# Summing the adaLN modulation on ScalarE and GpSimd instead of TensorE, inside the mixers of a two-layer hybrid trunk

## The chip, the cores and the metric

The kernel runs on one core of a Trainium2 chip. Its time is the device time of one execution in microseconds, the median of three runs. A core has TensorE (PE, matrix products; PEld is its loading of weights), VectorE (DVE), ScalarE (ACT), GpSimd (POOL) and SyncE (SP), which here issues the large DMAs. Each engine takes its own instructions in order and waits on semaphores of the others.

## The reference

Two residual layers over a sequence of 256 tokens of width 1024, in fp32, one sequence. Each layer is a mixer (attention of two head groups, one output projection) and a grouped top-2 mixture of 16 experts. Both sub-layers are modulated by a vector c, the same for all tokens:

```
m = silu(c) @ ada_w[layer] + ada_b[layer]          # 1024 x 6144 weights a layer
shift_m, scale_m, gate_m, shift_f, scale_f, gate_f = split(m, 6)
h = rmsnorm(x, norm_mix[layer]) * (1.0 + scale_m) + shift_m
x = x + gate_m * mixer(h)
h = rmsnorm(x, norm_ffn[layer]) * (1.0 + scale_f) + shift_f
x = x + gate_f * grouped_moe(h, ...)
```

The change is about the first line: a product of one row with a 1024 x 6144 matrix, 25 MB of weights a layer, each number of which is used once.

## The kernel before, in words

The program is one long list of instructions for each engine, written by Python generators that take turns, and ordered by a scheduler at build time. It goes through mixer 0, experts 0, mixer 1, experts 1.

The modulation is cut into *parts*. A part is two tiles of 1 MB of `ada_w` (128 partitions x 2048 fp32), loaded by SP into `slot`s, a ring of ten 1 MB tiles that all weights share. `n` is 2 for a shift with its scale (four parts) and 1 for a gate (two parts). The input index is 8 p + k: partition p holds eight rows k of the matrix, and `csil[:, k, 0]` holds silu(c) for them.

Before, `ada_part` gives each part to TensorE: eight matmuls (L340) with one useful column of weights (32 wide, so that four of them stand side by side in the array) and 512 moving columns, accumulated in a PSUM bank, which VectorE then adds to the tile `adac` (L349). `ada_end` closes a sum: for a gate two matmuls spread it over the partitions (L307) and it is added to `GATE`; for a shift and scale eight small matmuls (L313) bring it into columns `MOD` of 128 partitions.

`fill(n)` runs whole parts on the spot (at the start, between the layers, and in the experts). `ada_steps(n, rest)` does them inside a mixer in small steps: it loads one part ahead, lets `rest` steps pass, and then does a part. The attention loop `attend` calls `between()` once in each of its stages, which takes 4 or 5 such steps. There are ten parts in mixer 0 (the gate of its own output, shift and scale of the experts, shift and scale of mixer 1) and four in mixer 1.

In the same stages the side work goes on: projections `proj_t`, `proj_r` (L529 to L531), each k step of which needs a row of weights split into a high and a low part `hl`: ScalarE casts (L514), VectorE or GpSimd subtracts (L471). Then comes the output projection `out_proj`, whose result is added to the residual X (L710, L711). The attention itself uses VectorE for the row minimum (L576) and for weighting (L612, L614), ScalarE for the exponentials (L601).

The router at the start of `moe` finds the experts' order `ex_p`; SP reads it and only then can load the weights of all experts but the first ones.

Of the kernel before, what the change touches and what calls it, by code (L numbers as in the profile page):

```python
# [10 lines left out]
F32 = mybir.dt.float32  # L11
# [12 lines left out]
CAP = 64  # L24
# [83 lines left out]
def trunk(ctx, tc, ins, out):  # L108
# [218 lines left out]
    def ada_part(layer, v, n, j, W):  # L327
# [22 lines left out]
        if j == 2 * n - 1:  # L350
            yield
            ada_end(layer, v, n, sums.pop())

    def fill(n=1):
        for _ in range(n):
            if fills:
                at = fills.pop(0)
                W = first.pop(0) if first else ada_load(*at)
                for _ in ada_part(*at, W):
                    pass  # L360

    def ada_steps(n, rest):

        todo = [fills.pop(0) for _ in range(n)]
        W = ada_load(*todo[0])
# [141 lines left out]
    parts, low = [None], [vec]  # L507
    flop = [0]

    def split(row, n, view=None):  # L510

        t = parts[0].tile([P, 2, 512], F32R, name="hl", tag="hl", bufs=4)
        for src, hi, lo in [(row, t[:, 0, :n], t[:, 1, :n])] if view is None else view(row, t[:, 0, :n], t[:, 1, :n]):
            act.copy(hi, src)  # L514
            flop[0] ^= 1
            split_sub(low[0] or (vec, pool)[flop[0]], lo, src, hi)
        return t[:, 0, :n], t[:, 1, :n]
# [178 lines left out]
            vec.reciprocal(r, r)  # L696
            return [r[:, t:t + 1] for t in range(2)]

    def out_proj(OT, k0, W, engines, norm=None):

        gate = GATE[2]
        o2 = hp.tile([P, 4, 2, S], F32R, name="o2", tag="HT")
        for k in range(4):
            act.copy(o2[:, k, 0, :], OT[:, k0 + k, :])
            split_sub(engines[0], o2[:, k, 1, :], OT[:, k0 + k, :], o2[:, k, 0, :])

        def add(half, t, b):
            sl = slice(half * 512, half * 512 + 512)
            tmp = parts[0].tile([P, 512], F32, tag="tmp", name="tmp")
            vec.tensor_tensor(tmp, b, gate[:, sl], ALU.mult)  # L710
            engines[1].tensor_tensor(X[:, t, sl], X[:, t, sl], tmp, ALU.add)  # L711
            if norm is not None:
                norm.square(t, half)

        for half in range(2):
            outs = [bank("mm", [P, 512]) for _ in range(2)]

            def part(k, t, w):
                mm3(outs[t], [o2[:, k, i, t * P:(t + 1) * P] for i in range(2)], w, k == 0, k == 3)
            sl = slice(half * 512, half * 512 + 512)  # L720
            if half and norm is not None:

                ws = [split(W[k][:, sl], 512) for k in range(4)]
                for t in range(2):
                    for k in range(4):
                        part(k, t, ws[k])
                        yield
                    add(half, t, outs[t])
                continue
            for k in range(4):  # L730
                w = split(W[k][:, sl], 512)
                for t in range(2):
                    part(k, t, w)
                yield
            for t in range(2):
                add(half, t, outs[t])
            if norm is not None and half == 0:
                warm(AF.Sqrt, X[:, 0])


    def even_mixer(big, OT, banks):
# [28 lines left out]
        with scope("evw", 1) as wk:  # L770
# [15 lines left out]
            for i in range(2):  # L786
# [8 lines left out]
                xp = wk.tile([P, 16, 2, 16], F32, tag=f"xp{i}", name="xp")  # L795
# [40 lines left out]
            h1 = wk.tile([32, 512], F32, tag="xp0", name="h1")  # L836
# [137 lines left out]
    def moe(cp, wk, layer, norm, end):  # L974
# [353 lines left out]


        NR = 7  # L1330
        XG_x = cp.tile([P, 8, CAP], F32, name="XG_x")
        w_x = cp.tile([P, 1], F32, name="w_x")
        OT_x = cp.tile([P, 2, 2, P], F32R, name="OT_x")
        sides = [slice(0, 64), slice(64, 128)]

        def x_hidden(XG, W):
# [8 lines left out]
            return hid  # L1345

        def x_slots(o, w):
            def put(tt, wb):
# [3 lines left out]
            by_slot(o, w, 1, put)  # L1352

        def x_transposed(XG, hid):
            hT = XG[:, 4:8, :]
# [5 lines left out]
            act.copy(hT, tb)  # L1361
            return hT

        def x_down(hT, Wd):
            v, yg = row_tiles()
            y = bank("o", [P, 512])
            for k, row in enumerate(Wd):
# [45 lines left out]
        def rounds():  # L1413
# [23 lines left out]
            here, tmp = (cp.tile([P, NR, 16], F32, tag=n, name=n) for n in ("here", "here_t"))  # L1437
            vec.tensor_tensor(here, wide(before), rn, ALU.is_le)
            vec.tensor_tensor(tmp, wide(upto), rn, ALU.is_gt)
            vec.tensor_tensor(here, here, tmp, ALU.mult)  # L1440
# [25 lines left out]
                for i in range(n):  # L1466
                    yield t[:, i, :]

        def round_(i, space, o, XG):

            e = load_value(ex_x[:, i:i + 1], [ET.Pool], NE - 1)
            pick(o, at_x[:, :, i:i + 1].to_broadcast([P, 2, 2]), CAP)
            gather(XG, CAP, o)
            hid = x_hidden(XG, [streamed(nm, e, 8, space) for nm in ("moe_w_gate", "moe_w_up")])
            x_slots(o, wt_x[:, :, i:i + 1])
            for f in x_down(x_transposed(XG, hid), streamed("moe_w_down", e, 4, space)):
                f()

        def rest():
            space = hp.tile([P, 2048], F32, tag="HT", name="space")  # L1480
            o = pick_tile()[:, :, 0:2 * CAP]
            n = load_value(ex_x[:, NR:NR + 1], [ET.PE, ET.Activation, ET.DVE, ET.Pool], NR)

            def go(i):
                if i < NR:
                    with tc.If(n >= i + 1):
                        round_(i, space, o, XG_x)
# [5 lines left out]
        for h in range(2):  # L1493
            vec.tensor_scalar(OT_x[:, h], ident.unsqueeze(1).to_broadcast([P, 2, P]), 0.0, None, ALU.mult)
        then = picked([1, 2], placed[:, 0:2])
        before = None
        for i in range(len(GROUPS)):
# [76 lines left out]
    def odd_mixer(big, wk, OT, banks, CT, CM):  # L1574
# [24 lines left out]

        def put_c(t, b):  # L1600
            evac(VS[:, 0, t, :], b[:, 384:512])
            cl = wk.tile([P, 384], F32, tag="cl", name="cl")
# [153 lines left out]
    with scope("hl0", 2) as parts[0]:  # L1756
        with scope("ev", 1) as e1:
            bias_line()
            banks = norm_transposed()
            fill(4)  # L1760
            ada.add(ada_steps(10, 9))
            OT = new_ot()
            even_mixer(e1, OT, banks)
        wB = load_rows(ins["ev_w_out"][0][512:1024])
# [1 line left out]
        fills += parts_of(0, 5, 1)  # L1766
        norm = Norm()
        router_weights(0)
        run(out_proj(OT, 4, wB, (vec, vec), norm))
    experts(0, norm)  # L1770
    fills += parts_of(1, 2, 1) + parts_of(1, 3, 2)
    fill(2)
    ada.add(ada_steps(4, 9))
    with scope("hl1", 2) as parts[0]:
        with scope("od", 1) as e1, scope("odw", 2) as e2:
            CT, CM, KT[2] = carve((3, S), (256,), (768,))
# [6 lines left out]
        fills += parts_of(1, 5, 1)  # L1783
        norm = Norm()
        router_weights(1)
        run(out_proj(OT, 4, wB, (vec, vec), norm))
    experts(1, norm, Final())


# [23 lines left out]
```

## Time and profile before

| what | us |
|---|---|
| median of 3 runs (range) | 831.33 (828.41 to 831.84) |
| profiled execution | 828.97 |
| its span, first to last instruction | 827.3 |
| TensorE / VectorE / ScalarE / GpSimd busy | 730.9 / 379.0 / 233.7 / 101.0 |
| until 86 us: first modulation, first projections of layer 0 | 86.0 |
| 86 to 201.5: attention and output projection of layer 0 | 115.5 |
| 201.5 to 224: router of layer 0 | 22.5 |
| 224 to 470: experts of layer 0 | 246.0 |
| 470 to 574: mixer 1 | 104.0 |
| 574 to 593: router of layer 1 | 19.0 |
| from 593: experts of layer 1, final norm | 234.3 |

The stages were cut where the instructions of a stage begin. A stage in which one engine is busy nearly all the time goes at that engine's pace; a stage in which the DMA queues move their full rate goes at theirs. A row of the groups reads: line, engine, operation, tile written <- tiles read, shape, count | busy time, mean of one | idle time before it and who ended it.

### The profile page before, as it was taken

What the parts mean: (1) busy time and instruction counts of PE and PEld (TensorE: products, weight loads), DVE (VectorE), ACT (ScalarE), POOL (GpSimd) and SP (SyncE); (2) the same over time, 40 slices, a digit from 0 to 9 for tenths busy, and PEclk for the clock granted to TensorE, in tenths of its full rate; (3) what the DMA queues carried; (4) which work ended last, traced back from release to release, by engine and by line L of the source; (5) the groups of instructions that cost most, each with busy time, mean ns of one, the idle gap of its engine ahead of it and who ended that gap; (6) DMA issues with size and microseconds to landing.
All of it is one profiled execution on the core that took longest, in us unless ns stands there. A gap on an engine that the chain in (4) does not pass through costs nothing. (4 is left out here: it accounts for less than half of the span.)

```text
span 827.3 us, 12080 instructions
## 1 busy us (share of the span) xinstructions
PE 730.9 (88%) x4435; PEld 376.0 (45%) x4435; DVE 379.0 (46%) x1099; ACT 233.7 (28%) x565; POOL 101.0 (12%) x94
## 2 busy tenths in 40 slices
PE   4599999999799997899887899969899988899886
PEld 2298765557433342234222568547443332233223
DVE  2585777777841240312305754885931230322214
ACT  2264555545411110001012455544310110011012
POOL 1020211132200000000001223353100000000001
PEclk9899999999799998999999999998799998999998
DMA  9999878598399999999999987747399999999992
GB/s 355 339 372 418 316 255 256 221 419 321 131 426 374 426 427 424 426 426 427 427 426 414 374 338 210 279 172 279 117 426 377 427 426 423 426 425 428 422 414 91
DMA packets 68457, 291.15 MB, mean 352 GB/s; under 512 B 9174, under 2 KB 23202, under 8 KB 42530
## 3 DMA queue, kind: packets, MB, share of 16 engines
q1 hardware_dynamic: 64048, 283.53, 86.0%
q0 software_dynamic: 1152, 4.21, 1.3%
q10 hardware_dynamic: 3186, 2.51, 0.9%
q8 instruction: 39, 0.64, 0.3%
q14 instruction: 32, 0.26, 0.1%
HBM read 289.16 MB, written 1.06 MB: 351 GB/s over the span
## 5 line engine op out<-in xcount | busy, mean ns | idle before, releaser
L1091 PE MATMUL mm<-slot,XG 128*32 128x512 f32 (+1 forms) x464 | 107.6, 643 | 12.3 <-DMA slot<-in_moe_w_down_dram 6.3
L1091 PE MATMUL o<-slot,hT 128*32 128x512 f32 (+2 forms) x480 | 88.6, 589 | 2.5 <-DMA slot<-in_moe_w_down_dram 2.5
L1118 DVE TENSOR_TENSOR hq<-sc,hid 128x512 f32<-128x512 f32 x14 | 14.7, 1049 | 151.5 <-PE sc L1091 151.5
L514 ACT CAST hl<-slot 128x512 fp32r<-128x512 f32 (+2 forms) x112 | 60.9, 557 | 72.3 <-PE mm L531 41.8
L471 POOL TENSOR_TENSOR hl<-slot,hl 128x512 fp32r<-128x512 f32 x40 | 52.8, 1323 | 158.8 <-ACT hl L514 145.2
L1091 PE MATMUL sc<-slot,XG 128*32 128x512 f32 (+1 forms) x344 | 72.1, 593 | 0.0
L1091 PE MATMUL sc<-room,XG 128*32 128x512 f32 (+1 forms) x296 | 60.7, 593 | 1.2 <-DMA room<-in_moe_w_up_dram 1.2
L1091 PEld LDWEIGHTS mm<-slot,XG 128*32 128x32 f32 (+1 forms) x464 | 27.7, 129 | 69.3 <-issue 67.3
L529 PE MATMUL mm<-HH,hl 128*128 128x256 f32 x176 | 54.2, 310 | 4.7 <-ACT HH L503 4.7
L1162 DVE SCALAR_TENSOR_TENSOR adac<-o,w,GATE 128x512 f32<-128x512 f32 (+1 forms) x29 | 21.2, 732 | 79.0 <-PE o L1091 77.7
L1144 ACT CAST yg<-adac 128x512 fp32r<-128x512 f32 (+1 forms) x28 | 17.1, 612 | 137.9 <-DVE adac L1162 137.9
L1091 PE MATMUL mm<-room,XG 128*32 128x512 f32 (+1 forms) x176 | 52.8, 678 | 0.0
L531 PE MATMUL mm<-HH,hl 128*128 128x256 f32 x176 | 50.0, 286 | 0.8 <-DVE hl L471 0.8
L530 PE MATMUL mm<-HH,hl 128*128 128x256 f32 x176 | 50.2, 287 | 0.0
L471 DVE TENSOR_TENSOR hl<-slot,hl 128x512 fp32r<-128x512 f32 (+2 forms) x72 | 43.3, 623 | 13.5 <-ACT hl L514 13.2
L1091 PE MATMUL o<-room,hT 128*64 128x512 f32 (+2 forms) x176 | 47.4, 577 | 2.2 <-DMA room<-in_moe_w_down_dram 2.0
L340 PE MATMUL tp<-slot,csil 128*32 128x512 f32 x344 | 45.5, 611 | 3.3 <-DMA slot<-in_ada_w_dram 3.1
L1151 PE MATMUL tp<-yg,OT 128*128 128x512 f32 (+1 forms) x112 | 38.1, 441 | 11.1 <-DVE X L1152 5.2
L1073 PE MATMUL tp<-pick,XH 128*128 128x256 f32 (+1 forms) x128 | 39.8, 333 | 8.1 <-DVE XG L1077 4.7
L1152 DVE TENSOR_TENSOR X<-X,tp 128x512 f32<-128x512 f32 (+1 forms) x56 | 36.1, 674 | 17.4 <-PE tp L1151 17.1
L1075 ACT ACTIVATE XG<-tp,mod,mod 128x256 f32<-128x256 f32 (+1 forms) x32 | 17.2, 538 | 94.9 <-PE tp L1073 94.9
L1091 PEld LDWEIGHTS o<-slot,hT 128*32 128x32 f32 (+1 forms) x480 | 24.9, 119 | 40.8 <-issue 34.2
(372 smaller groups left out, 1272.6 us busy)
## 6 DMA issues: line engine op xcount, KB each, us to landing
slot<-in_moe_w_gate_dram SPq DMA_DIRECT2D x48, 1024.0 KB, 13.4
slot<-in_ada_w_dram SPq DMA_DIRECT2D x43, 1024.0 KB, 10.2
slot<-in_moe_w_down_dram SPq DMA_DIRECT2D x42, 1024.0 KB, 19.4
slot<-in_moe_w_up_dram SPq DMA_DIRECT2D x35, 1024.0 KB, 14.4
room<-in_moe_w_up_dram SPq DMA_DIRECT2D x27, 1024.0 KB, 10.1
room<-in_moe_w_down_dram SPq DMA_DIRECT2D x18, 1024.0 KB, 15.3
room<-in_moe_w_gate_dram SPq DMA_DIRECT2D x16, 1024.0 KB, 12.2
slot<-in_ev_w_in_dram SPq DMA_DIRECT2D x8, 1024.0 KB, 8.3
```

The lines of the kernel that those rows point to most:

```text
L340: last[0] = mm(b[32 * g:32 * g + 32], csil[:, k, :], W[i][:, g, :], start=i == 0, stop=i == 1)
L471: return eng.tensor_tensor(lo, v, hi.bitcast(F32), ALU.subtract)
L514: act.copy(hi, src)
L529: mm(o, a[0], b[0], start=start, stop=False, skip_group_check=True)
L530: mm(o, a[0], b[1], start=False, stop=False, skip_group_check=True)
L531: mm(o, a[1], b[0], start=False, stop=stop, skip_group_check=True)
L1073: mm(b, xk[i][:, t, k, :], o[:, t, 0:n], start=t == i == 0, stop=t == i == 1)
L1075: act.activation(XG[:, k, :], b, AF.Identity, bias=sh[:, k:k + 1], scale=fa[:, k:k + 1])
L1091: last[0] = mm(*args, **kw)
L1151: mm(cb, OT[:, t, :], x, start=i == 0, stop=i == 1)
L1152: vec.tensor_tensor(X[:, t, sl], X[:, t, sl], cb, ALU.add)
L1162: vec.scalar_tensor_tensor(v, y, w, gate[:, sl], ALU.mult, ALU.mult)
```

## The change

Inside the mixers, `ada_steps` calls a new function `ada_acc` instead of `ada_part`. ScalarE multiplies each 128 x 1024 row of the tile by its silu(c), one number a partition, in place (the first row of a sum goes into the new tile `acc`); GpSimd adds the scaled row to `acc` in two halves of 512. When a sum is complete, TensorE sums `acc` over the partitions: two matmuls with a tile of ones for a gate, sixteen with one column of ones for a shift and scale. `rest` goes from 9 to 6, since a part now takes four steps. `fill`, which does the other parts, stays as it was.

`acc` is 8 KB a partition in the pool of the split tiles. To make room, `hl` has 3 buffers instead of 4 (the fourth of the last output projection comes from a pool `more` that is opened for it), `xp` and `h1` of mixer 0 lie in the still unused output tile OT, `cl` has one buffer, and tiles of the overflow rounds (`XG_x`, `OT_x`, `here`) come from existing working tiles; `OT_x` is set to zero in each round instead of at the start of each expert stage.

```diff
+    def ada_acc(layer, v, n, j, W, state):
+        if j == 0:
...
+            state[:] = [parts[0].tile([P, 2, D], F32, tag="acc", name="acc", bufs=1)]
+        acc, rows = state[0], 3 - n
+        for i, t in enumerate(W):
+            t = t.rearrange("p a b -> p (a b)").rearrange("p (r a b) -> p r a b", r=rows, a=n)
+            for r in range(rows):
+                k = rows * (2 * j + i) + r
+                for a in range(n):
+                    x, c = t[:, r, a], csil[:, k, 0:1]
+                    act.activation(acc[:, a] if k == 0 else x, x, AF.Copy, scale=c)
+                    if k:
+                        for sl in (slice(0, 512), slice(512, D)):
+                            pool.tensor_tensor(acc[:, a, sl], acc[:, a, sl], x[:, sl], ALU.add)
+                    yield
+        if j < 2 * n - 1:
+            return
+        yield
+        yield
+        if n == 1:
...
+                mm(b, ONES, acc[:, 0, sl], start=True, stop=True)
+                vec.tensor_tensor(GATE[v][:, sl], GATE[v][:, sl], b, ALU.add)
+            return
+        b = bank("tp", [P, 2, 8])
+        for a in range(2):
+            by = acc[:, a].rearrange("p (m k) -> p k m", k=8)
+            for k in range(8):
+                mm(b[:, a, k:k + 1], by[:, k, :], ONES[:, 0:1], start=True, stop=True)
...
-            yield from ada_part(*at, W)
+            yield from ada_acc(*at, W, state)
...
-        t = parts[0].tile([P, 2, 512], F32R, name="hl", tag="hl", bufs=4)
+        t = (pool_ or parts[0]).tile([P, 2, 512], F32R, name="hl", tag="hl", bufs=1 if pool_ else 3)
...
-            ada.add(ada_steps(10, 9))
+            ada.add(ada_steps(10, 6))
...
-    ada.add(ada_steps(4, 9))
+    ada.add(ada_steps(4, 6))
```

How the program moves, at three places. On GpSimd, in mixer 0, from the first split of the attention on, there stood before (each row an instruction, xN for N in a row; `scc` belongs to the compressed branch):

```order
L471 TENSOR_TENSOR hl<-slot,hl 128x512
L876 MEMSET scc 128x128 x2
L471 TENSOR_TENSOR hl<-slot,hl 128x512 x11
L711 TENSOR_TENSOR X<-X,tmp 128x512 x2
L471 TENSOR_TENSOR hl<-slot,hl 128x512 x2
L711 TENSOR_TENSOR X<-X,tmp 128x512 x2
L471 TENSOR_TENSOR hl<-slot,hl 128x512 x2
```

On GpSimd, in mixer 0, there stand now (the lines are 43 further on; L372 is the new addition), first and, after a part left out that goes on in the same way, last before the final sum is taken:

```order
L372 TENSOR_TENSOR acc<-acc,slot 128x512 x2
L920 MEMSET scc 128x128 x2
L514 TENSOR_TENSOR hl<-slot,hl 128x512
L372 TENSOR_TENSOR acc<-acc,slot 128x512 x4
L514 TENSOR_TENSOR hl<-slot,hl 128x512
L372 TENSOR_TENSOR acc<-acc,slot 128x512 x8
...
L514 TENSOR_TENSOR hl<-slot,hl 128x512
L754 TENSOR_TENSOR X<-X,tmp 128x512 x2
L372 TENSOR_TENSOR acc<-acc,slot 128x512 x8
L514 TENSOR_TENSOR hl<-slot,hl 128x512
L372 TENSOR_TENSOR acc<-acc,slot 128x512 x6
```

Seventy additions in all stand between the same splits, which wait behind them in GpSimd's queue.

On TensorE, at the end of the last of mixer 0's three sums, there stood before (`o_1709` and `o_2045` are the inputs of the two output projections):

```order
L340 MATMUL tp<-slot,csil 32x512 x8
L529 MATMUL mm<-hl,o_1709 128x512
...
L529 MATMUL mm<-hl,o_1709 128x512
L313 MATMUL tp<-K_105,adac 64x4 x8
L624 MATMUL tp<-K_105,St 128x128 x4
L530 MATMUL mm<-hl,o_1709 128x512
L531 MATMUL mm<-hl,o_1709 128x512
L674 MATMUL sc<-sw_2040,ONES 128x16
L529 MATMUL mm<-hl,o_2045 128x512
```

There stand now:

```order
L677 MATMUL o<-PT,room 64x128 x2
L389 MATMUL tp<-ONES,acc 128x1 x8
L667 MATMUL tp<-K_105,St 128x128 x2
L389 MATMUL tp<-ONES,acc 128x1 x8
L572 MATMUL mm<-hl,o_1720 128x512 x2
...
L667 MATMUL tp<-K_105,St 128x128 x2
L572 MATMUL mm<-hl,o_2067 128x512
```

The sum's end stays in front of the second output projection, now with sixteen matmuls that read what GpSimd has added.

On GpSimd, in mixer 1, there stood before:

```order
L471 TENSOR_TENSOR hl<-slot,hl 128x512 x15
L711 TENSOR_TENSOR X<-X,tmp 128x512 x2
L471 TENSOR_TENSOR hl<-slot,hl 128x512 x4
L711 TENSOR_TENSOR X<-X,tmp 128x512 x2
L471 TENSOR_TENSOR hl<-slot,hl 128x512 x5
```

There stand now, until the sum is complete:

```order
L514 TENSOR_TENSOR hl<-slot,hl 128x512
L372 TENSOR_TENSOR acc<-acc,slot 128x512 x4
L514 TENSOR_TENSOR hl<-slot,hl 128x512 x2
L372 TENSOR_TENSOR acc<-acc,slot 128x512 x14
L514 TENSOR_TENSOR hl<-slot,hl 128x512 x2
L372 TENSOR_TENSOR acc<-acc,slot 128x512 x2
L514 TENSOR_TENSOR hl<-slot,hl 128x512
...
L372 TENSOR_TENSOR acc<-acc,slot 128x512 x2
```

Eighteen additions stand before the two splits with which the attention's side projection starts.

## Rows read from the trace of the kernel before

**Rows 1.** Busy time by stage, all engines; below the heading, one row a stretch.

```profile
core 0: us, PE busy (x) PEld busy (x) DVE busy (x) ACT busy (x) POOL busy (x), PEclk, DMA share, GB/s
86.00:201.50 115.50, 114.24 (x704) 71.89 (x703) 87.36 (x314) 61.88 (x185) 25.59 (x21) 1.00 0.79 289
224.00:470.00 246.00, 215.52 (x1268) 84.62 (x1268) 78.60 (x179) 36.20 (x68) 10.01 (x18) 0.97 1.01 414
481.00:531.00 50.00, 49.12 (x314) 33.98 (x306) 26.61 (x88) 23.61 (x64) 18.03 (x14) 1.00 0.73 240
550.00:560.00 10.00, 6.26 (x31) 4.25 (x30) 9.44 (x23) 3.98 (x13) 6.45 (x5) 0.92 0.32 106
```

**Rows 2.** Waits of SP's queue, 200 to 240 us: total us, times, longest.

```profile
SPq L1376 <- DVE ex_p L1405: 20.8, 1, 20.8
```

**Rows 3.** The same by stretch for L340 alone: stretch, PE, PEld, clock, DMA.

```profile
86.00:201.50 115.50, 20.69 (x160) 4.09 (x160) 1.00 0.79 289
470.00:532.00 62.00, 8.11 (x64) 1.46 (x64) 1.00 0.78 276
```

**Rows 4.** VectorE's L349 alone by stretch: stretch, busy, clock, DMA.

```profile
86.00:201.50 115.50, 7.00 (x7) 1.00 0.79 289
481.00:531.00 50.00, 3.16 (x3) 1.00 0.73 240
```

**Rows 5.** TensorE in order of time: start, us, then the instructions.

```profile
184.40 1.07 PE L313 MATMUL tp<-K,adac 128*64 128x4 f32 x16 [0.16 <-DVE adac L349]
...
530.01 1.09 PE L313 MATMUL tp<-K,adac 128*64 128x4 f32 x16
```

**Rows 6.** Groups of one line and shape: busy us, mean ns | idle before.

```profile
L514 ACT CAST hl<-slot 128x512 fp32r<-128x512 f32 x88 | 53.6, 616 | 65.8 <-PE mm L531 39.1 <-DMA slot<-in_ev_w_in_dram 12.9 <-issue 6.4
...
L711 POOL TENSOR_TENSOR X<-X,tmp 128x512 f32<-128x512 f32 x8 | 10.2, 1283 | 8.9 <-DVE tmp L710 4.5 <-DVE r L610 2.6 <-DVE sne L1706 0.9
...
L992 PE MATMUL sc<-RWF,xT 128*128 128x16 f32 x64 | 9.6, 290 | 0.5 <-ACT xT L990 0.5
...
L1137 PE MATMUL tp<-placed,pick 128*128 128x2 f32 x40 | 5.1, 231 | 0.0
...
L996 ACT ACTIVATE XH<-X,rsx 128x1024 fp32r<-128x1024 f32 x2 | 4.1, 2067 | 0.0
```

**Rows 7.** GpSimd in order of time, layer 1.

```profile
502.28 2.71 POOL L471 TENSOR_TENSOR hl<-slot,hl 128x512 fp32r<-128x512 f32 x2 [15.06 <-ACT hl L514]
...
536.97 2.50 POOL L711 TENSOR_TENSOR X<-X,tmp 128x512 f32<-128x512 f32 x2 [0.90 <-DVE l L1722]
539.43 1.26 POOL L471 TENSOR_TENSOR hl<-slot,hl 128x512 fp32r<-128x512 f32 x1
```

**Rows 8.** ScalarE in order of time: one row of each layer.

```profile
81.27 0.62 ACT L840 ACTIVATE g<-g 32x512 f32<-32x512 f32 x1
...
485.74 0.37 ACT L1617 COPY raw<-mm 128x256 f32<-128x256 f32 x1
```

**Rows 9.** VectorE in order of time, both layers.

```profile
100.71 0.83 DVE L916 TENSOR_TENSOR l<-l,pads 128x2 f32<-128x2 f32 x1
...
188.83 1.67 DVE L614 TENSOR_SCALAR St<-St,r 128x256 f32<-128x256 f32 x2
...
537.55 0.72 DVE L1717 TENSOR_TENSOR l<-l,sne 128x2 f32<-128x2 f32 x1
538.19 2.58 DVE L614 TENSOR_SCALAR St<-St,r 128x128 f32<-128x128 f32 x2
...
545.44 0.08 DVE L576 DVE_READ_ACCUMULATOR2_ANT mx<- 128x1 f32 x1
545.44 0.16 DVE L1717 TENSOR_TENSOR l<-l,sne 128x2 f32<-128x2 f32 x1
...
546.54 0.48 DVE L614 TENSOR_SCALAR St<-St,r 128x128 f32<-128x128 f32 x2
```

**Rows 10.** VectorE's L614, then L471, alone, 86 to 201.5 us.

```profile
86.00:201.50 115.50, 17.85 (x48) 1.00 0.79 289
...
86.00:201.50 115.50, 13.88 (x24) 1.00 0.79 289
```

More of the change, by code (lines that the diff above doesn't have):

```diff
@@ L352, in ada_part @@
             ada_end(layer, v, n, sums.pop())
+    def ada_acc(layer, v, n, j, W, state):
+        if j == 0:
+            if n == 1:
+                GATE[v] = big.tile([P, D], F32, name="GATE", tag="GATE")
+                pool.dma_start(GATE[v], ins["ada_b"][layer:layer + 1, v * D:(v + 1) * D].to_broadcast([P, D]))
+            state[:] = [parts[0].tile([P, 2, D], F32, tag="acc", name="acc", bufs=1)]
[15 more added lines that the diff above has]
+        yield
+        if n == 1:
+            for half in range(2):
+                b = bank("tp", [P, 512])
+                sl = slice(half * 512, half * 512 + 512)
+                mm(b, ONES, acc[:, 0, sl], start=True, stop=True)
[6 more added lines that the diff above has]
+                mm(b[:, a, k:k + 1], by[:, k, :], ONES[:, 0:1], start=True, stop=True)
+        for a in range(2):
+            o = MOD[layer, v + a]
+            vec.tensor_tensor(o, b[:, a], ADC[:, layer, v + a, :], ALU.add)
+            if a:
+                vec.scalar_tensor_tensor(o, o, 1.0, NRM[:, (v // 3) * 2 + layer, :], ALU.add, ALU.mult)
     def fill(n=1):
@@ L508, in trunk, with split @@
     flop = [0]
-    def split(row, n, view=None):
-        t = parts[0].tile([P, 2, 512], F32R, name="hl", tag="hl", bufs=4)
+    def split(row, n, view=None, pool_=None):
+        t = (pool_ or parts[0]).tile([P, 2, 512], F32R, name="hl", tag="hl", bufs=1 if pool_ else 3)
         for src, hi, lo in [(row, t[:, 0, :n], t[:, 1, :n])] if view is None else view(row, t[:, 0, :n], t[:, 1, :n]):
@@ L721, in out_proj @@
             if half and norm is not None:
-                ws = [split(W[k][:, sl], 512) for k in range(4)]
+                ws = [split(W[k][:, sl], 512, pool_=more if k == 3 else None) for k in range(4)]
                 for t in range(2):
@@ L1347, in x_slots @@
         def x_slots(o, w):
+            OT_x = wk.tile([P, 2, 512], F32R, tag="yg", name="yg")[:, 0, :].rearrange("p (h t s) -> p h t s", h=2, t=2)
+            for h in range(2):
+                vec.tensor_scalar(OT_x[:, h], ident.unsqueeze(1).to_broadcast([P, 2, P]), 0.0, None, ALU.mult)
             def put(tt, wb):
@@ L1352, in x_slots @@
             by_slot(o, w, 1, put)
+            return OT_x
         def x_transposed(XG, hid):
@@ L1362, in x_transposed, with x_down @@
             return hT
-        def x_down(hT, Wd):
+        def x_down(hT, Wd, OT_x):
             v, yg = row_tiles()
@@ L1436, in rounds @@
             rn = number.unsqueeze(2).to_broadcast([P, NR, 16])
-            here, tmp = (cp.tile([P, NR, 16], F32, tag=n, name=n) for n in ("here", "here_t"))
+            t = ada_tile()
+            here, tmp = (t[:, 16 * NR * n:16 * NR * (n + 1)].rearrange("p (r e) -> p r e", e=16) for n in range(2))
             vec.tensor_tensor(here, wide(before), rn, ALU.is_le)
@@ L1474, in round_ @@
             hid = x_hidden(XG, [streamed(nm, e, 8, space) for nm in ("moe_w_gate", "moe_w_up")])
-            x_slots(o, wt_x[:, :, i:i + 1])
-            for f in x_down(x_transposed(XG, hid), streamed("moe_w_down", e, 4, space)):
+            OT_x = x_slots(o, wt_x[:, :, i:i + 1])
+            for f in x_down(x_transposed(XG, hid), streamed("moe_w_down", e, 4, space), OT_x):
                 f()
@@ L1768, in trunk @@
         router_weights(0)
-        run(out_proj(OT, 4, wB, (vec, vec), norm))
+        with scope("hm0", 1) as more:
+            run(out_proj(OT, 4, wB, (vec, vec), norm, more))
     experts(0, norm)
@@ L1785, in trunk @@
         router_weights(1)
-        run(out_proj(OT, 4, wB, (vec, vec), norm))
+        with scope("hm1", 1) as more:
+            run(out_proj(OT, 4, wB, (vec, vec), norm, more))
     experts(1, norm, Final())
```

18 lines of the change are left out of this document (8 added, 10 removed).

## The prediction

> **What bounds the kernel now.** I read the busy times by stage first. From 86 to 201.5 us (attention of layer 0, its side projections and output projection) TensorE is busy 114.2 of 115.5 us at the full clock, while VectorE is busy 87.4, ScalarE 61.9 and GpSimd 25.6; from 481 to 531 us, in layer 1, TensorE is busy 49.1 of 50 us [rows 1]. So TensorE sets the pace of the mixers. From 224 to 470 us the DMA queues move 414 GB/s: the experts wait for weights [rows 1]. What joins the two is the SP queue's longest wait there: 20.8 us for `ex_p`, the routed expert numbers, which come out of the mixer [rows 2]. All expert loads that need no routing had been issued before that wait began. A microsecond by which a mixer ends earlier or later therefore arrives at the end of the span unchanged, twice over (one for each layer).
>
> **What is removed.** Fourteen parts leave TensorE's partial sums (L340): ten in layer 0's mixer, 20.7 us of TensorE's time, and four in layer 1's, 8.1 us [rows 3]. VectorE loses the additions at L349: seven, 7.0 us, and three, 3.2 us [rows 4].
>
> **What is added on TensorE.** At the end of each shift-and-scale sum, 8 matmuls of the old form took 1.07 to 1.09 us [rows 5]; now 16 with 128 columns of weights and one column of data, 32 records, as an fp32 matmul stands twice in the trace. A like one (L1137, two columns) takes 5.1 us / 40 = 0.13 us, and L992 with 16 columns 9.6 / 64 = 0.15 [rows 6]: 2.1 us (half of L1137's, for a weight load that overlaps) to 4.8. I take L1137's: 32 x 0.13 = 4.1, 3.0 more than before, twice in layer 0 and once in layer 1. The gate's end stays two 512-wide matmuls. If TensorE went on setting the pace, that would be -20.7 + 6.0 = -14.7 and -8.1 + 3.0 = -5.1 us.
>
> **What is added on ScalarE.** 4 x 14 = 56 scalings of 128x1024, 40 of them in layer 0. A 128x512 cast takes 53.6 / 88 = 0.61 us; a 128x1024 activation with a strided side takes 2.07 [rows 6]. A contiguous one is bounded by one cast and by 2.07; I take two casts, 1.22 us less the overlap of successive instructions, about 1.1. Layer 0: 61.9 + 44 = 106 us. That fits into a phase that is longer than 115 us, not into one of 100: ScalarE alone would eat most of TensorE's gain. It also gets a new wait: the first row of a sum is scaled into `acc`, which has one buffer, so it waits until TensorE has taken the sum before, and exponentials of the attention queue behind it. While TensorE reads a sum as soon as GpSimd has it, this costs at most the idle time that I allow below.
>
> **What is added on GpSimd.** 70 additions of 128x512 in layer 0, 28 in layer 1 (every row but the first of each sum, two halves each). The same instruction on the same kinds of operands, L711, takes 1.283 us [rows 6], and two in a row 2.50 [rows 7]. This is the largest term. In layer 0 the first addition can start when ScalarE has scaled two rows after the tanh that ends at 81.9 us [rows 8], with one cast between them: 81.9 + 2 x 1.1 + 0.6, about 84.6. From there to the last addition GpSimd's program holds 70 additions, 12 splits `hl`, 2 additions to X and two short memsets: 84 x 1.28 + 0.4 = 107.9 us. Without one idle moment the last sum is ready at 192.5 us. The TensorE matmuls that take it stand in front of the last six matmuls of the first output projection's half and of the whole second one; their predecessors began at 184.40 [rows 5], and what followed them took until 201.5. TensorE takes instructions in order, so this gate moves by +8.1 us, and the mixer's end by 8.1 + 3.0 = +11.1. GpSimd, idle for 90 of 115 us now, is the new bound.
>
> Layer 1 by the same steps: the first rows can be scaled behind the copy at L1617, which ends at 486.1 [rows 8], and a cast; additions start at about 487.8. 28 additions and 8 splits until the sum is complete: 36 x 1.28 = 46.1, so 533.9, against 530.01 for the old end [rows 5]: +3.9, with the longer end +6.9. Within that, the splits which began at 502.28 [rows 7] stand behind 18 additions and 2 other splits: 487.8 + 20 x 1.28 = 513.4. TensorE, 98% busy there, waits for them about 10 us; its relief of 5 us pays half of it.
>
> **What it does to VectorE.** GpSimd's instructions hold up VectorE's. A pair of L614 takes 0.48 us alone (546.54) but 2.58 at 538.19, while three GpSimd instructions run back to back from 536.97 to 540.69, and L1717 0.72 instead of 0.16 [rows 7, 9]: 2.1 + 0.57 = 2.67 us of waiting, 0.89 for each GpSimd instruction. Instructions that read PSUM don't show it. Around single ones it is less: of the 19 GpSimd tensor instructions from 100 to 196 us, ten lie over a stretched VectorE instruction (the first L916 at 100.71, 0.83 us; the last the L614 pair at 188.83, 1.67 [rows 9]), together 7.9 us, 0.42 each. The additions come in runs of 2 to 12, broken by waits for ScalarE; I take the middle, 0.65. Layer 0: 87.4 - 7.0 + 70 x 0.65 = 126 us of VectorE's time in a phase that GpSimd alone makes 126.6 long. No engine in a chain of dependent steps is 100% busy: in the stretch which already looks like this, 550 to 560 us, GpSimd is at 65%, VectorE at 94% and TensorE at 63% [rows 1]. At 92% the phase is 137 us, +21.5. With 0.42 it stays at +11; with 0.89, 143 / 0.92 = 155, +40. Layer 1 has VectorE at 53% [rows 1]; 26.6 - 3.2 + 28 x 0.65 = 42 us don't fill the 57 us that GpSimd makes it. There I add 3 us of idle time to the 6.9: +10 (6.9 to 17: at the upper end the 10 us for the late splits come on top unpaid).
>
> The Trainium skill (SBUF — State Buffer, section "SBUF: two separate sides") calls the port that GpSimd shares with VectorE an exclusive lock, held for a whole instruction, which a VectorE instruction with two SBUF inputs needs too. By that the two times would add up with nothing beside each other, which speaks against moving sums to GpSimd; the trace agrees on who waits, but the two L711 still took 2.50 us with L614 waiting beside them, so the other direction is not seen here.
>
> **The small edits.** The two fills of `OT_x` leave the start of each expert stage: like the L614 pair, 0.48 us each layer, on VectorE before `ex_p`: -1 us in all. `hl` has 3 buffers for 4: in the first projections ScalarE's casts wait for a buffer in any case; 0 here, up to +2 where a cast comes later. The new places of `xp`, `h1`, `here` and the round's tiles carry the same instructions: 0. The rounds themselves don't run in this trace. SP's order is the same but for one tile of ada weights; slots are freed later by GpSimd, which the 20.8 us before `ex_p` cover: 0.
>
> **Sum.** The profiled execution took 828.97 us, 1.7 more than its span, and 2.4 below the median of 831.33. 829 + 21.5 + 10 - 1 = 859.5: I forecast 860 us, some 31 over the profiled run, about 29 over the median.
>
> **The rivals.**
> - Queue alone: GpSimd's length counts, VectorE's waits hide in its free 24%. 829 + 11.1 + 6.9 - 1 = 846. For it: the low 0.42 for single instructions. Against: the runs of additions.
> - Strict exclusion: GpSimd and VectorE's L614 and L471 never overlap. GpSimd until its last split: 70 + 17 + 4 = 91 x 1.28 = 117 us; L614 and L471 17.9 + 13.9 [rows 10], less 3 of waits in them, 29. 84.6 + 146 + 3 is 234, +32; layer 1 at its upper end, +17: 829 + 49 - 1 = 877. Against: the undelayed L711 pair.
> - Faster: TensorE keeps the pace, 829 - 14.7 - 5.1 - 1 = 808. It decides where an addition costs less than (184.40 - 17.7 - 84.6) / 84 = 0.98 us (17.7: the 20.7 less the first longer end). For it: GpSimd is at 22% in the mixer now. Against: the shortest pair of L711 took 2.50 [rows 7], 1.25 each.
> - No change: the experts' transfers hide the mixers' end. 829. Against: the 20.8 us in which SP holds for `ex_p`.
>
> **How the numbers follow.** The forecast 0.48 (its own range 851 to 870), queue alone 0.26, strict exclusion 0.15, faster 0.06, no change 0.05. The range of eight in ten reaches from a little under the queue's 846 to a little over the 877: 842 to 882. About 0.5% (4 us) is what the measurement can tell from no change: faster 0.06, same 0.06, slower 0.88.
>
> **What would show it.** In the profile after: GpSimd busy over 80% of the attention of layer 0, its additions at 1.28 to 1.4 us each; TensorE with idle time that ends on `hl` or `acc` of GpSimd; L614 and L612 on VectorE well over their present means; the wait for `ex_p` ending some 20 us later in layer 0 and 30 us later in layer 1; both expert stages as long as now. Wrong: additions of 1 us or less, or TensorE still 98% busy with a mixer that ends before 195 us.

## The result and the profile after

The changed kernel took 892.32 us (median of 4 runs, 890.96 to 893.26) against 831.59 for the kernel before (4 runs, 828.41 to 832.14): ratio 1.075, 95% interval [1.073, 1.078], 61 us slower. The forecast was 860, at most 882. The direction and the engine to blame were right, the size was about half.

Where the 61 us lie is read from one instruction on VectorE, the cast that writes `ex_p` once in each layer and so ends the mixer for SP's queue. Of the kernel before and of the changed kernel (durations in ns, first and last start in us):

```profile
L1405 DVE CAST ex_p<-placed x2: 164/164/164, 222.3 to 591.7; 1x13 int32<-1x13 f32 x2
```

```profile
L1452 DVE CAST ex_p<-placed x2: 163/164/164, 272.3 to 655.5; 1x13 int32<-1x13 f32 x2
```

Layer 0 loses 50.0 us, layer 1 13.8 (383.2 from cast to cast instead of 369.4), and what follows the last cast is as long as before (236.1 us now, 235.6 before). I had +20 and +10. The two profiled runs lie 64 us apart, the medians 61. One profiled run differs from the next by some 3 us at this cast (the run with the small edits alone, below, has it at 225.1, and 373.7 for layer 1, with an unchanged median): 3 to 4 us are the error of all sums made from these times.

Layer 0's mixer in the changed kernel, to the point 50 us later than the end of the first stretch of [rows 1]:

```profile
core 0: us, PE busy (x) PEld busy (x) DVE busy (x) ACT busy (x) POOL busy (x), PEclk, DMA share, GB/s
86.00:251.50 165.50, 131.44 (x593) 94.25 (x592) 121.51 (x307) 98.96 (x224) 116.92 (x92) 0.82 0.60 211
```

TensorE, 99% busy before, has 34 us of idle time in a longer phase and runs at a granted clock of 0.82 instead of 1.00. VectorE's time is 121.5 us, close to the 126 forecast, but it fills 73% of the phase, not 92%. GpSimd fills 71%, not over 80%. No engine is full. The groups of the additions and of the weighting on VectorE (`L657`), by line, and the latter in the kernel before (`L614`):

```profile
L372 POOL TENSOR_TENSOR acc<-acc,slot 128x512 f32<-128x512 f32 x98 | 127.2, 1330 | 37.1 <-ACT slot L369 30.4
...
L657 DVE TENSOR_SCALAR St<-St,r 128x128 f32<-128x128 f32 (+1 forms) x72 | 55.7, 805 | 0.8
```

```profile
L614 DVE TENSOR_SCALAR St<-St,r 128x128 f32<-128x128 f32 (+1 forms) x72 | 29.8, 454 | 0.7
```

An addition takes 1.33 us, and VectorE is held up as foreseen. What was not foreseen stands in GpSimd's and TensorE's own waits of this mixer, 84 to 226 us (releaser, total us, times, longest), in TensorE's order around the first and the last end, and in GpSimd's last stretch:

```profile
engine line waited for: us in total, times, longest us
POOL acc L372 <- ACT slot L369: 30.4, 6, 22.4
POOL hl L514 <- ACT hl L557: 18.1, 4, 13.1
POOL acc L372 <- issue: 6.7, 2, 3.5
```

```profile
PE tp L667 <- DVE St L657: 9.9, 12, 2.7
PE mm L573 <- POOL hl L514: 7.4, 5, 2.6
PE mm L573 <- DVE hl L514: 4.9, 4, 1.5
PE tp L389 <- POOL acc L372: 3.5, 2, 2.2
```

```profile
166.15 3.97 PE L389 MATMUL tp<-ONES,acc 128*128 128x1 f32 x16 [1.27 <-POOL acc L372]
170.04 1.12 PE L674 MATMUL o<-PT,room 128*64 128x256 f32 x4
170.95 0.64 PE L677 MATMUL o<-PT,room 128*64 128x128 f32 x4
171.52 3.97 PE L389 MATMUL tp<-ONES,acc 128*128 128x1 f32 x16
...
225.38 3.97 PE L389 MATMUL tp<-ONES,acc 128*128 128x1 f32 x16 [2.24 <-POOL acc L372]
229.21 0.67 PE L667 MATMUL tp<-K,St 128*128 128x128 f32 x2
229.67 3.79 PE L389 MATMUL tp<-ONES,acc 128*128 128x1 f32 x16
```

```profile
185.37 7.99 POOL L372 TENSOR_TENSOR acc<-acc,slot 128x512 f32<-128x512 f32 x6 [1.07 <-ACT slot L369]
193.33 1.26 POOL L514 TENSOR_TENSOR hl<-slot,hl 128x512 fp32r<-128x512 f32 x1
194.55 10.56 POOL L372 TENSOR_TENSOR acc<-acc,slot 128x512 f32<-128x512 f32 x8
...
219.16 1.26 POOL L514 TENSOR_TENSOR hl<-slot,hl 128x512 fp32r<-128x512 f32 x1
220.38 7.41 POOL L372 TENSOR_TENSOR acc<-acc,slot 128x512 f32<-128x512 f32 x6
227.75 1.26 POOL L514 TENSOR_TENSOR hl<-slot,hl 128x512 fp32r<-128x512 f32 x1
```

The 22.4 us lie before the first addition. After it GpSimd still stands idle for 8.0 + 18.1 + 6.7 = 33 us: 26 of them it waits for ScalarE's scalings and casts, and for the 6.7 the profile names no releaser. From 185.4 to 229.0 us it then runs without an idle moment. The last sum, forecast for 192.5 us "without one idle moment", is complete at 227.8, and TensorE begins on its first half at 225.4. TensorE waits in turn for VectorE and for GpSimd's splits, in small pieces, and hardly for the sums themselves (3.5 us). The first end takes 7.9 us, not 4.1.

### The profile page after: what moved, and what is told of

Same layout as the page of the kernel before. It is cut to its first block, busy times and chain, and to the rows that moved or that the text cites. A ratio compares the mean times of both kernels' runs of the same rounds, so it can differ in the third digit from the quotient of the medians.

```text
span 891.6 us, 11915 instructions
## 1 busy us (share of the span) xinstructions
PE 755.9 (85%) x4259; PEld 409.2 (46%) x4259; DVE 423.3 (47%) x1079; ACT 285.3 (32%) x617; POOL 225.8 (25%) x192
## 5 line engine op out<-in xcount | busy, mean ns | idle before, releaser
L372 POOL TENSOR_TENSOR acc<-acc,slot 128x512 f32<-128x512 f32 x98 | 127.2, 1330 | 37.1 <-ACT slot L369 30.4
L1595 POOL TENSOR_TENSOR XO<-X,FN 128x512 f32<-128x512 f32 (+1 forms) x4 | 3.9, 1003 | 235.6 <-DVE X L1196 235.6
L574 PE MATMUL mm<-HH,hl 128*128 128x256 f32 x176 | 52.4, 302 | 8.5 <-POOL hl L514 6.7
L514 DVE TENSOR_TENSOR hl<-slot,hl 128x512 fp32r<-128x512 f32 (+2 forms) x72 | 48.1, 697 | 19.6 <-ACT hl L557 17.8
L572 PE MATMUL mm<-HH,hl 128*128 128x256 f32 x176 | 54.1, 310 | 3.8 <-ACT HH L546 3.8
L657 DVE TENSOR_SCALAR St<-St,r 128x128 f32<-128x128 f32 (+1 forms) x72 | 55.7, 805 | 0.8
L369 ACT ACTIVATE slot<-slot,csil 128x1024 f32<-128x1024 f32 x49 | 54.4, 1143 | 0.0
L573 PE MATMUL mm<-HH,hl 128*128 128x256 f32 x176 | 52.4, 300 | 0.0
```

Of the source, the lines that this page charges most:

```text
L369: act.activation(acc[:, a] if k == 0 else x, x, AF.Copy, scale=c)
L372: pool.tensor_tensor(acc[:, a, sl], acc[:, a, sl], x[:, sl], ALU.add)
L514: return eng.tensor_tensor(lo, v, hi.bitcast(F32), ALU.subtract)
L572: mm(o, a[0], b[0], start=start, stop=False, skip_group_check=True)
L573: mm(o, a[0], b[1], start=False, stop=False, skip_group_check=True)
L574: mm(o, a[1], b[0], start=False, stop=stop, skip_group_check=True)
```

## The experiments

Of each run: the time and its ratio to the kernel before on the same chip, when layer 0's `ex_p` is written (222.3 before, 272.3 after), and the time from there to layer 1's (369.4, 383.2). Where a form computes another modulation, and with it another routing, it ran once, and only the time of layer 0's `ex_p` is read.

| run | us | ratio [95%] | layer 0 | layer 1 |
|---|---|---|---|---|
| small edits alone | 832.3 | 1.002 [0.999, 1.005] | 225.1 | 373.7 |
| old end | 889.5 | 1.071 [1.069, 1.073] | 270.5 | 382.6 |
| filler on TensorE | 904.6 | 1.090 [1.087, 1.093] | 276.0 | 392.5 |
| gate only | 845.3 | 1.018 [1.016, 1.020] | 236.9 | 370.6 |
| unread additions | 938.5 | 1.132 [1.128, 1.136] | 304.6 | 396.8 |
| unread scalings | 842.5 | 1.014 [1.011, 1.017] | 230.2 | 376.8 |
| no additions | 841.4 (one run) | | 234.6 | |
| no scalings | 1096.9 (one run) | | 281.7 | |
| additions on VectorE | 871.3 | 1.051 [1.047, 1.054] | 257.4 | 377.4 |
| fused on VectorE | 870.9 | 1.051 [1.048, 1.054] | 255.7 | 378.1 |
| splits on VectorE | 884.8 | 1.067 [1.064, 1.070] | 268.3 | 382.1 |
| no additions, old end | 824.5 (one run) | | 221.0 | |
| fused, old end | 858.8 | 1.035 [1.032, 1.037] | 244.4 | 378.1 |
| side-by-side weights | 951.4 (one run) | | 267.1 | |
| three steps apart | 901.8 | 1.087 [1.084, 1.090] | 279.6 | 384.3 |
| nine steps apart | 902.4 | 1.088 [1.082, 1.094] | 276.0 | 385.8 |

**Small edits alone.**

```
-            yield from ada_acc(*at, W, state)
+            yield from ada_part(*at, W)
-            ada.add(ada_steps(10, 6))
+            ada.add(ada_steps(10, 9))
```

> The small edits alone (the new places of xp, h1 and OT_x, three hl buffers, the extra hl buffer in the second output projection); the modulation stays on TensorE as before. My theory and all the rivals that lay the loss on the moved sums: within 3 us of the kernel before, the -1 us of the prediction included, ex_p of layer 0 written at 222 us and of layer 1 at 591. Rival 'small edits': a missing hl buffer or the split into an extra pool holds the projections up, and more than 10 of the 61 us show up here.

No difference that can be measured. The loss belongs to the moved sums.

**The old end.** My first theory after the result was the end: 7.9 us, with ScalarE idle 9.4 and GpSimd 13.1 behind it.

```
-                mm(b[:, a, k:k + 1], by[:, k, :], ONES[:, 0:1], start=True, stop=True)
+            last[0] = mm(b[32 * g:32 * g + 32], ONES[:, 0:32], acc[:, g // 2, (g % 2) * 512:(g % 2) * 512 + 512], start=True, stop=True)
+        act.copy(t.rearrange("p (k m) -> p m k", k=8), b.rearrange("p (m k) -> p m k", k=8))
+        yield
+        ada_end(layer, v, n, t)
```

> The changed kernel with another end of each shift-and-scale sum: four 512-wide matmuls with ONES as weights, one ScalarE copy, and the eight small matmuls of the kernel before, about 2.1 us of TensorE instead of 16 matmuls in 7.5 to 8 us. My theory (the new end is the mis-sized term: it holds TensorE, and through the single acc buffer ScalarE 9.4 us and GpSimd 13.1 us, and the clock is at half after it): 892 falls to 866 to 874, ex_p of layer 0 from 272 to 255, GpSimd without the 13 us gap at 168 to 183. Rival 'GpSimd's additions and VectorE's waits set the pace': only the ends on the path get shorter, 5.8 us in layer 0 and 5.8 in layer 1, about 880, with the GpSimd gap filled by other waits.

Only 3 us came back. The theory fell as stated, and the rival's 880 was too low as well: other waits filled the gap.

**Filler on TensorE.** For each of the 28 tiles a bundle of four 512-wide matmuls on constants, whose result nobody reads:

```
+            mm(b[32 * g:32 * g + 32], csil[:, 0, :], ONES.unsqueeze(1).to_broadcast([P, 4, P]), start=True, stop=True)
```

> The changed kernel with 28 bundles of four 512-wide matmuls on constants added (one for each loaded tile), whose results nobody reads: TensorE gets about as much to do in the mixers as it had before. Theory 'clock': TensorE at half clock (96 to 100, 168 to 180, 208 to 236 us) stretches its part of the chain; with the dense filler the granted clock of the mixer goes from 0.83 to over 0.95 and the time falls to 870 to 882. Rival 'the low clock only follows from TensorE's waits': the filler (28 x 1 us) goes into idle time or adds to the path, 892 to 905.

12 us slower. The mixer's granted clock rose from 0.82 to 0.89 only, and the mixer still ended 3.7 us later. The filler neither kept the clock up nor bought time, so the low clock reads as a companion of the waits; that a full clock would give nothing isn't shown.

**Gate only.**

```
+            yield from (ada_acc(*at, W, state) if at[2] == 1 else ada_part(*at, W))
```

> ScalarE and GpSimd sum only the gate of layer 0 (14 scalings of 128x1024 less two, 14 additions, ended by two 512-wide matmuls); the shift and scale sums stay on TensorE as before. By my prices: TensorE loses two parts, 4.1 us, at the start of the mixer where GpSimd has 14 additions of 1.3 us to do in free time and VectorE waits 14 x 0.65 = 9 us less the 1 us of additions it loses, in 24% free time: 827 if the waits hide, 836 if they lie on the path. If every part moved costs its share of the 50 us of layer 0 (a fifth), +10: 841.

14.6 us in layer 0 for 14 additions; 845.3 is over all three estimates. The additions run between 87 and 115 us; `rest` is 6 here too, so that the parts left on TensorE come closer together than before. 90 to 110 us in the kernel before and in this one:

```profile
90.00:110.00 20.00, 19.60 (x137) 12.71 (x136) 15.70 (x62) 9.45 (x32) 3.58 (x3) 1.00 0.74 284
```

```profile
90.00:110.00 20.00, 14.33 (x84) 11.50 (x83) 19.49 (x53) 11.10 (x33) 14.75 (x12) 0.87 0.51 185
```

VectorE goes from 79% to 97% busy while it finishes 53 instructions instead of 62; TensorE, its customer, finishes 84 instead of 137, of which 32 were the gate's own parts. VectorE's "24% free time" was an average over 115 us and not there.

**Unread additions, unread scalings.** The modulation stays on TensorE; one side of the new work is done beside it on a tile that nobody reads.

```
+                for sl in (slice(0, 512), slice(512, D)):
+                    pool.tensor_tensor(a[:, sl], a[:, sl], b[:, sl], ALU.add)
```

> The modulation stays on TensorE as in the kernel before (with the small edits); beside it GpSimd makes 112 additions of 128x512 at the places of the changed kernel's 98, on a tile that nobody reads, and ScalarE scales nothing. What GpSimd's instructions do to the rest is left by itself. Theory 'VectorE held up, and hl queued on GpSimd, lie on the chain of the attention': TensorE has its 28.8 us of parts too, so the loss is at least what the changed kernel lost and may be more, 885 to 910, ex_p of layer 0 at 265 or later. Rival 'ScalarE's scalings in front of the exponentials': 832 to 850, ex_p at 222 to 232. Rival 'the sums that are waited for (gates on acc)': nobody waits here, 840 to 860.

```
+                act.activation(a, b, AF.Copy, scale=csil[:, 0, 0:1])
```

> As the run before, but ScalarE's 56 scalings of 128x1024 instead of the additions, into a tile that nobody reads; GpSimd adds nothing. Theory 'ScalarE': 56 x 1.14 = 64 us stand in ScalarE's queue ahead of exponentials and casts that others wait for; 860 or more, ex_p of layer 0 at 245 or later. Theory 'GpSimd and VectorE': ScalarE has 46% free time, 832 to 845, ex_p at 222 to 233.

The scalings cost 10 us over the small edits alone (842.5 against 832.3), the additions 106. But neither kept to the changed kernel's times. Waiting for no data, all 40 scalings of layer 0 ran between 14 and 83 us and all its 80 additions between 4 and 138 us, before the attention began. The row minimum with which the attention starts, in the kernel before and with the unread additions:

```profile
L576 DVE CUSTOM_DVE_ANT_0 St<-sc,room x72: 272/350/425, 87.0 to 550.8; 128x128 f32<-128x128 f32 x36, 128x256 f32<-128x256 f32 x36
```

```profile
L627 DVE CUSTOM_DVE_ANT_0 St<-sc,room x72: 275/352/426, 169.0 to 657.5; 128x128 f32<-128x128 f32 x36, 128x256 f32<-128x256 f32 x36
```

82.0 of the 82.3 us that layer 0 lost were lost before the attention. So neither run is a measure of what the changed kernel's scalings or additions cost inside it. What the additions did to the first projections is seen in GpSimd and VectorE:

```profile
20.32 52.14 POOL L420 TENSOR_TENSOR acc<-acc 128x512 f32<-128x512 f32 x42
...
117.57 20.50 POOL L420 TENSOR_TENSOR acc<-acc 128x512 f32<-128x512 f32 x14
```

```profile
22.73 1.02 DVE L514 TENSOR_TENSOR rsx<-ssx 128x2 f32<-128x2 f32 x1
23.78 48.71 DVE L515 TENSOR_SCALAR rsx<-rsx 128x2 f32<-128x2 f32 x1
72.76 0.17 DVE L517 RECIPROCAL rsx<-rsx 128x2 f32<-128x2 f32 x1 [0.27 <-ACT rsx L516]
```

An instruction on 128x2 elements stood for 48.7 us, until the additions ended. Beside the later row of 14 additions no VectorE instruction took longer than 1.5 us, and in the changed kernel, while GpSimd ran from 185.4 to 229.0 us without an idle moment, none longer than 1.8. So a row without gaps is not enough for the long wait, and what was needed besides stays open.

**No additions; no scalings.** The first leaves out the 98 additions, the second the 49 scalings of later rows, so modulation and routing are others and only layer 0's `ex_p` is read.

```
-                            pool.tensor_tensor(acc[:, a, sl], acc[:, a, sl], x[:, sl], ALU.add)
```

> The changed kernel without its 98 additions: each sum holds only its first scaled row, so the modulation, and with it the routing, is another; read is the time at which layer 0's ex_p is written (272.3 in the changed kernel, 222.3 before), which no routing precedes. Theory 'GpSimd and VectorE': TensorE's relief of about 15 us shows, 208 to 228. Rival 'ScalarE': 245 to 265.

```
-                    act.activation(acc[:, a] if k == 0 else x, x, AF.Copy, scale=c)
+                    if k == 0:
+                        act.activation(acc[:, a], x, AF.Copy, scale=c)
```

> The changed kernel without the 49 scalings of the later rows: GpSimd adds the rows as loaded, so the modulation and the routing are others; read is layer 0's ex_p (272.3 in the changed kernel). Theory 'GpSimd and VectorE': additions wait for the load alone, 255 to 270. Rival 'ScalarE': 222 to 245.

Without additions 37.7 of the 50 us are gone, but 234.6 lies between the two ranges. Without scalings it got 9.4 us later, against both theories. GpSimd still waits for ScalarE there, 17 us after its first addition for the first rows, which ScalarE scales into `acc`, and 23.5 for casts; why the mixer got longer stays open. To take ScalarE's scalings away brought nothing here.

**Additions on VectorE; scaling and addition fused there.**

```
-                            pool.tensor_tensor(acc[:, a, sl], acc[:, a, sl], x[:, sl], ALU.add)
+                            vec.tensor_tensor(acc[:, a, sl], acc[:, a, sl], x[:, sl], ALU.add)
```

> The changed kernel with its 98 additions of 128x512 on VectorE instead of GpSimd; ScalarE's scalings and the ends as they are. VectorE gets about 98 x 0.7 = 69 us of work of its own, more than the 54 us by which GpSimd stretched it, but no splits stand behind additions on GpSimd and none holds the shared port. Theory 'VectorE's time is the pace, however it is spent': 885 to 905. Theory 'what costs is GpSimd being slow (1.33 us an addition) and in the way of the hl splits': 845 to 870, ex_p of layer 0 at 235 to 255.

```
+                        vec.scalar_tensor_tensor(acc[:, a], x, c, acc[:, a], ALU.mult, ALU.add)
```

> The changed kernel with the scaling and the addition of each later row as one VectorE instruction (49 of 128x1024, some 1.1 to 1.4 us each by two L657-like halves of 0.7); GpSimd adds nothing, ScalarE scales the 7 first rows only. Theory 'VectorE's time': 49 x 1.3 = 64 us, like the run before, 880 to 905. Theory 'GpSimd's queue and ScalarE's': 840 to 865.

Both 871. By line, 84 to 240 us, first the additions, then the fused form:

```profile
L372 DVE TENSOR_TENSOR acc<-acc,slot 128x512 f32<-128x512 f32 x70 | 49.3, 730 | 0.0
```

```profile
L372 DVE SCALAR_TENSOR_TENSOR acc<-slot,csil,acc 128x1024 f32<-128x1024 f32 x35 | 49.1, 1408 | 0.7 <-ACT acc L370 0.7
```

With 49 us of work of VectorE's own, layer 0 is 15 to 17 us shorter than with the additions on GpSimd. Each theory had a part of it. The second form also takes the scalings of the later rows off ScalarE, for the same time on VectorE, and is 1.7 us shorter than the first: ScalarE's scalings cost little here.

**Splits on VectorE.**

```
-            split_sub(low[0] or (vec, pool)[flop[0]], lo, src, hi)
+            split_sub(vec, lo, src, hi)
```

> The changed kernel with all subtractions of the splits on VectorE, so that no split stands behind additions on GpSimd; VectorE gets some 17 x 0.7 = 12 us more in layer 0's mixer. Theory 'the splits queued on GpSimd': ex_p of layer 0 10 or more earlier than 272, 870 to 882. Theory 'VectorE's time': later by up to 12, 892 to 910.

4 us earlier in layer 0 although VectorE has the splits as well, 7.6 us in all: GpSimd's queue before `hl` is a part, and a small one; 884.8 lies between the two ranges.

**No additions and the old end; fused and the old end.** The edits of both.

> The run without additions with the kernel before's small matmuls as the end of each sum (2.1 us of TensorE instead of 7.5 to 8): sums of the first rows only, so modulation and routing are others; read is ex_p of layer 0, 234.6 with the new end. If the new ends are what eats TensorE's relief there: 216 to 226. If ScalarE's scalings are: 230 to 235.

> The run with scaling and addition in one VectorE instruction, and the small matmuls of the kernel before as the end of each sum. The new end cost 13.6 us of layer 0 where nobody added (234.6 against 221.0) and 1.8 where GpSimd added (272.3 against 270.5). If it is hidden by GpSimd's lateness alone: 10 or more less than 870.9 in layer 0 and some 4 in layer 1, 853 to 860, ex_p of layer 0 at 242 to 246. If VectorE's chain hides it as well: 864 to 870. If layer 1 (ex_p to ex_p, 369.4 before) comes out shorter than before, that layer alone is worth the change.

The new ends cost 13.6 us where nobody adds (234.6 to 221.0), 11.3 where VectorE adds (255.7 to 244.4), and 1.8 where GpSimd adds. They are real, and with GpSimd adding they are hidden. Even with no additions at all layer 0 is no more than some 1 to 4 us shorter than before, so in this arrangement the idea can bring little. ScalarE is nearly full there from 100 to 160 us:

```profile
100.00:160.00 60.00, 54.51 (x307) 37.05 (x305) 45.27 (x184) 57.25 (x134) 10.45 (x8) 1.00 0.80 281
```

That this is what eats TensorE's relief isn't shown: the attention's last row minimum came 9.7 us earlier than before (177.7 against 187.4), and most of that was lost behind it. The mixer of the last form (fused, old end), to 201.5 + 22.1 us:

```profile
86.00:223.60 137.60, 109.33 (x572) 73.93 (x571) 123.31 (x346) 67.02 (x191) 29.81 (x22) 0.93 0.72 260
```

VectorE is 90% busy, and the phase comes to the 137 us of the forecast.

**Side-by-side weights.** The modulation comes out permuted.

```
-            by = acc[:, a].rearrange("p (m k) -> p k m", k=8)
+            by = acc[:, a].rearrange("p (k m) -> p k m", k=8)
```

> The changed kernel with the 128 weight columns of each of the end's 16 matmuls taken side by side instead of 8 elements apart; the modulation comes out permuted, so the routing is another; read is the time of the 32 records of an end. If the stride of the weights makes them slow: 32 x 0.13 = 4.2 us at the full clock instead of 7.5 to 8. If it is the fp32 weight load of 128 columns itself, or the clock: 7.5 to 8 as now.

```profile
164.82 1.05 PE L389 MATMUL tp<-ONES,acc 128*128 128x1 f32 x8
166.05 1.08 PE L389 MATMUL tp<-ONES,acc 128*128 128x1 f32 x8 [0.17 <-POOL acc L372]
167.06 1.12 PE L674 MATMUL o<-PT,room 128*64 128x256 f32 x4
167.96 0.64 PE L677 MATMUL o<-PT,room 128*64 128x128 f32 x4
168.53 3.57 PE L389 MATMUL tp<-ONES,acc 128*128 128x1 f32 x16
```

Both halves are true. 0.13 us a record while the clock is full, as `L1137` said [rows 6], and 0.22 after it has fallen behind the first half. With the stride it is 0.25 at half clock, and in layer 1 0.24 as well, where the first 4 us were granted 1.00:

```profile
586.32 7.55 PE L389 MATMUL tp<-ONES,acc 128*128 128x1 f32 x32
```

```profile
586.00:590.00 4.00, 4.00 (x20) 3.96 (x18) 3.83 (x15) 2.52 (x8) 1.57 (x2) 1.00 1.03 404
590.00:594.00 4.00, 4.00 (x19) 4.00 (x19) 1.22 (x3) 0.00 (x0) 0.98 (x1) 0.52 1.01 412
```

**Closer together, further apart.**

```
-            ada.add(ada_steps(10, 6))
+            ada.add(ada_steps(10, 3))
```

> The changed kernel with three steps of the mixer instead of six between two parts of the modulation, so that the same scalings and additions stand closer together and earlier in the queues. Theory 'each addition costs its time wherever it stands, since additions and attention wait for one another': 885 to 900. Theory 'the last sum comes too late, the additions as such are covered': the last sum is ready some 20 us earlier, 870 to 882.

The second has 9 in place of 3.

> The changed kernel with nine steps of the mixer between two parts, as the kernel before had, instead of six: the same scalings and additions, further apart and later. With three steps it took 9.5 us more than with six. Theory 'additions close together hold VectorE up for longer, so spreading helps': 880 to 888. Theory 'the last sum is late': later still, 895 or more, since the last part starts some 30 steps later.

Both lose 10 us. With nine steps TensorE waits longer for the last sums themselves in layer 0 (3.5 us with six), though `ex_p` came only 3.7 us later there:

```profile
PE tp L389 <- POOL acc L372: 24.4, 2, 18.3
```

With three steps that wait is 6.7 us, and TensorE's for the normalised scores of VectorE is 16.9 instead of 9.9. Neither "dense is worse" nor "late is worse" alone holds; six steps lie between the two.

## Why the prediction was wrong

- **The step that failed** is "At 92% the phase is 137 us, +21.5". It put everything new side by side under one busy engine. Measured, the phase was 165.5 us, with VectorE busy for about the time forecast, but only 73% of the phase. The mixer without GpSimd's additions and with the old end (fused, old end) does come out at +22.1, VectorE at 90%; that the numbers agree is partly luck, since VectorE's 123 us there hold 49 us of fused additions, and the forecast's 126 held 70 x 0.65 = 45.5 us of waiting for GpSimd. In the changed kernel two more delays stand in line. Layer 0, from run to run: 222.3 to 244.4, the work on VectorE, +22.1; to 255.7, the new ends, +11.3; to 272.3, GpSimd and ScalarE doing it instead, +16.6. Layer 1: +8.7, 0, +5.1. Layer 1's 5.1 is hardly over the error of 3 to 4 us. The order of the steps matters (with GpSimd adding, the ends come to 1.8), so they are one way to read the 50 us and no separate prices. Taken out instead of replaced, the additions are worth 37.7 and the new ends 13.6 more: together all of the 50.
- **"Without one idle moment the last sum is ready at 192.5 us"** failed with it: 33 us of idle time, and the last sum at 227.8. The additions stand in program order between the steps of the attention, behind scalings that queue behind exponentials, and the attention waits for VectorE, which waits for the additions. The waits above are the links of such a ring, in which no engine is full; no run opened it at one link alone.
- **The end's price**, 4.1 us, was taken from a row with weights side by side and the clock full. Measured 7.9, 7.8 and 7.6. "This costs at most the idle time that I allow below" was wrong too: ScalarE stood idle for 9.4 us until the first end had read the one `acc` buffer. A second buffer wasn't tried.
- **Right**: an addition at 1.28 (1.33), a scaling at 1.1 (1.14), VectorE's time (126, measured 121.5), the small edits at nothing, the experts hiding nothing, and layer 1 (+13.8 in 6.9 to 17). "ScalarE alone would eat most of TensorE's gain" came out in its number (221.0 without additions and with the old end); its reason isn't shown.
- **Rivals**: "strict exclusion" came nearest, 877, and was short by 15; its reason, that VectorE's weighting and splits never run beside GpSimd, is not what the changed kernel shows: from 185.4 to 229.0 us GpSimd's 34 instructions took 1.28 us each, as `L711` before, while VectorE did 12 weightings and 3 splits.
- **Open**: what the scalings and the additions each cost inside the attention when nobody waits for them (the unread ones ran before it), why layer 0 got later without scalings, what share of the 16.6 us is `hl`'s queue (the 4 us above are net of VectorE's added splits), and what a full clock would give.

Of the forms that compute the same, none beats the kernel before; the nearest are the small edits alone (no difference) and the gate alone (+1.8%).

## What to carry to other kernels

Free time of an engine over a phase is not free where it is wanted: look at the windows in which the new work would run, for the engine itself and for those that share a port or a queue with it. When work moves from the bound engine to three others that feed each other, look for the delays that stand in line, and don't take the largest alone; here even the rival that added two of them up, 877, was short. New work that is run beside the old, unread, tests something only if it waits for the data that the real work waits for: look in the trace for where it ran before its time is read.

## What the runs showed of the hardware

- In the unread additions VectorE instructions took 48.7 us (on 128x2 elements), 13.2 and 9.0 us beside rows of GpSimd additions. Just before the longest, in the same row, one on 128x2 got through in 1.0 us; beside the later row of 14 the longest was 1.5 us; and in the changed kernel, where GpSimd ran 34 instructions from 185.4 to 229.0 us and 39 from 536.0 to 586.0 without an idle moment, 1.8. The Trainium skill (SBUF — State Buffer, section "SBUF: two separate sides") says that the engine that starts first has the shared port pair for its whole instruction. By that rule a wait would end with the addition under way, 1.25 us: the short waits agree, the three long ones lasted for many additions.
- 32 fp32 weight loads with columns 8 elements apart took 7.5 us at a granted clock that began at 1.00; side by side, 0.13 us each at the full clock. In both runs the granted clock went from full to half while, or right after, the one-column matmuls of the first end ran; at layer 0's last end in the changed kernel it had fallen at 221.5 us, before them.
- GpSimd slows VectorE down, and VectorE slows GpSimd down more rarely. The mean of `L657` is 805 ns, against 454 for `L614` before. The additions' median is 1.28 us, what `L711` took before [rows 6], but six of the 98 took 1.68 to 1.74 us, and each of these started while a split on VectorE ran (min/median/max in ns):

```profile
L372 POOL TENSOR_TENSOR acc<-acc,slot x98: 1255/1282/1744, 86.4 to 582.0; 128x512 f32<-128x512 f32 x98
```
